# High and low parts of a row in one 512-column product: every other up chunk of a second feed-forward

## Chip, core and metric

One core of a Trainium2 chip runs the whole program. The metric is device time in microseconds of one execution, as the median of several runs. The engines that matter here are TensorE (products, with a weight load ahead of each; PE and PEld in the profile), VectorE (DVE), ScalarE (ACT) and SyncE (SP), whose queue starts the loads from memory.

## What is computed

A decoder trunk of two layers on 256 positions of width 1024, in float32. Each layer has a token mixer and a gated feed-forward, both with a normalised and modulated input and a gated residual. The feed-forward, cut to what matters:

```python
def swiglu(h, w_gate_up, w_down):           # 1024 -> 2 x 2816 -> 1024
    g, u = jnp.split(h @ w_gate_up, 2, axis=-1)
    return (jax.nn.silu(g) * u) @ w_down

h = modulate(x, norm_ffn[i], sh_f, sc_f)    # rms_norm(x) * (1 + scale) + shift
x = x + g_f[:, None, :] * swiglu(h, w_gate_up[i], w_down[i])
```

Layer 0 has an attention as its mixer, layer 1 a short gated convolution. The change is in the feed-forward of layer 1, called `f1` in the tiles' names.

## The kernel before

Everything lies with features on the 128 partitions and the 256 positions along a row (`S = 256`); the width of 1024 is 8 blocks k (`KD = 8`) of 128. To keep float32 precision on an engine format with fewer bits, each operand is split into a high part (rounded copy, ScalarE, L98 for weights) and a low part (the remainder, VectorE, L99). A product of weights and rows is then three products into one accumulator, `mm3`: high weights with high rows (L254), high weights with low rows (L255), low weights with high rows (L258). Each has its own weight load of 128x128 and moves 256 columns.

Weights come in chunks of 256 output columns. `prep` loads a chunk into one of five `wf` buffers and splits it into `wh` and `wl`, of which there are three each; `get` runs two chunks ahead of the products, so the split of a chunk waits until an older chunk's products are done. Between the weight chunks `ada_piece` computes modulation vectors on VectorE (L109). A scheduler sets the order of the instructions on each engine from the code's order and from the priorities; SyncE's queue takes the loads in the code's order.

The feed-forward, `ffn(l, norm, av, done)`, runs over 11 chunks j of 256 hidden features. For j = 0 gate and up run together from a row that isn't normalised yet (`raw_gemm`); its up accumulators are the two PSUM banks tagged "alt", its gate accumulators two of the four tagged "gemm". For j = 1 to 10, `feat_gemm` gives the gate accumulator `pg` and then the up accumulator `pu`, each 8 k x 2 halves o x 3 products, one bank of 2 x 256 columns. ScalarE takes the silu of `pg` (L456), VectorE multiplies it with `pu` (L458), and `split` stores high and low parts in `a1h` and `a1l` (L405, L406). `out_proj` then makes the down products `op_d`: 8 accumulators x 22 blocks x 3 products. Residuals and stores follow.

The rows that gate and up products read are `hs`, a pair of tiles for high and low parts with rows 1 KB apart. `new_pair("h", ...)` takes the pair anew for each of the four norms (`m0`, `f0`, `m1`, `f1`), in the same two places.

Two things stand ahead of the plain chunks of some stages: `settle` issues two tiny bfloat16 products at the end of `raw_gemm`, and the argument `cuts` of `feat_gemm` divides some low-weight products of one chunk in two.

Of the kernel before, what the change touches and what calls it, by code (L numbers as in the profile page):

```python
# [8 lines left out]
F32 = mybir.dt.float32  # L9
F32R = mybir.dt.float32r  # L10
BF16 = mybir.dt.bfloat16
AF = mybir.ActivationFunctionType
# [3 lines left out]
P = 128  # L16
S = 256
D = 1024
KD = D // P
# [14 lines left out]
def trunk_kernel(ctx: ExitStack, tc: tile.TileContext, out_in, x_t, cols_in, scale_in, shift_in, ada_in, qk_rows, kv_in,  # L34
                 o_in, in_in, gu_in, down_in, out_f):
    nc = tc.nc
# [3 lines left out]
    act = ctx.enter_context(tc.tile_pool(name="act", bufs=1))  # L40
    tmp = ctx.enter_context(tc.tile_pool(name="tmp", bufs=2))
    psum = ctx.enter_context(tc.tile_pool(name="psum", bufs=1, space=bass.MemoryType.PSUM))

    def ps_gemm(name):
        return psum.tile([P, 2, CW], F32, tag="gemm", name=name, bufs=4)
# [7 lines left out]
    def ps_alt(name):  # L53
        return psum.tile([P, 512], F32, tag="alt", name=name, bufs=2)
# [90 lines left out]
    def room(tag, n, name, dtype=F32):  # L145
        size = {"al": KF * S + 16, "ah": KF * S, "zh": KD * (S + 32), "zl": KD * (S + 2)}.get(tag, KD * S)
        return act.tile([P, size], dtype, tag=tag, name=name)[:, 16 if tag == "al" else 0:][:, :n]

    def pair_rows(flat):
        return flat.rearrange("p (k s) -> p k s", s=S)  # L150

    def new_pair(tag, name, nk):
        return tuple(pair_rows(room(tag + p, nk * S, name + p, F32R)) for p in "hl")

    room("al", 1, "first_al")
    xT = act.tile([P, KD, S], F32, name="xT")
    hs = new_pair("h", "m0", KD)
    room("ah", 1, "first_ah")
    x_tok = room("zh", 2 * D, "x_tok").rearrange("p (t d) -> p t d", d=D)
    for t in range(2):  # L160
# [76 lines left out]
    def produce(upto):  # L237
        while pos[0] < len(chunks) and pos[0] <= upto:
            ch = chunks[pos[0]]
            if ch[0] == "a":  # L240
                ada_piece(*ch[1:])
            else:
                ready[ch[1]] = prep(ch[2], ch[3], "_".join(map(str, ch[1])), ch[1] in first_two)
            pos[0] += 1

    def get(key):
        n = place[key]
        produce(order[min(n + AHEAD, len(order) - 1)])
        return ready.pop(key)


    def mm3(ps, lhs, rhs, first, last, cut=0):
        (ah, al), (bh, bl) = lhs, rhs
        nc.tensor.matmul(ps, ah, bh, start=first, stop=False, skip_group_check=True)  # L254
        nc.tensor.matmul(ps, ah, bl, start=False, stop=False, skip_group_check=True)  # L255

        for a, b in ((0, cut), (cut, S)) if cut else ((0, None),):
            nc.tensor.matmul(ps[:, a:b], al, bh[:, a:b], start=False, stop=last, skip_group_check=True)  # L258

    def feat_gemm(parts, xs, nk, cuts=()):  # L260

        cuts = list(cuts)
        xh, xl = xs
        for k in range(nk):
            for ps, (wh, wl) in parts:
                for o in range(2):
                    cs = slice(o * P, (o + 1) * P)
                    mm3(ps[:, o], (wh[:, k, cs], wl[:, k, cs]), (xh[:, k], xl[:, k]),
                        k == 0 and o == 0, k == nk - 1, cuts.pop(0) if o and k % 2 and cuts else 0)

    def tok_gemm(parts, xs, nk, between={}):
        xh, xl = xs
        for k in range(nk):
            for fn, *args in between.get(k, ()):
                fn(*args)
            for ps, (wh, wl) in parts:
                for t in range(2):
                    ts = slice(t * P, (t + 1) * P)
                    mm3(ps[:, t], (xh[:, k, ts], xl[:, k, ts]), (wh[:, k], wl[:, k]),
                        k == 0 and t == 0, k == nk - 1)  # L280
# [6 lines left out]
    def wide_pair(name):  # L287
        flat = [room("z" + p, RAW, name + p, F32R) for p in "hl"]
        return (tuple(f[:, :KD * S].rearrange("p (k s) -> p k s", s=S) for f in flat),
                tuple(f.rearrange("p (k s) -> p k s", s=S + 2) for f in flat))  # L290
# [12 lines left out]
    def modulated_tile(hs, l, sh, scl, rows, k, name):  # L303
        t = tmp.tile([P, S], F32, tag="t", name="t_" + name, bufs=3)
        nc.vector.scalar_tensor_tensor(t, xT[:, k], mcol(l, scl, k), rows, op0=ALU.mult, op1=ALU.mult)
        nc.scalar.activation(hs[0][:, k], t, AF.Identity, bias=mcol(l, sh, k))
        nc.vector.scalar_tensor_tensor(hs[1][:, k], t, mcol(l, sh, k), hs[0][:, k].bitcast(F32),
                                       op0=ALU.add, op1=ALU.subtract)

    def modulated(l, sh, scl, rows, name):  # L310
        hs = new_pair("h", name, KD)
        for k in range(KD):
            modulated_tile(hs, l, sh, scl, rows, k, f"{name}_{k}")
        return hs
# [89 lines left out]
    def split(dst, k, src, name, psum_src=False):  # L404
        nc.scalar.activation(dst[0][:, k], src, AF.Copy)  # L405
        nc.vector.tensor_sub(dst[1][:, k], src, dst[0][:, k].bitcast(F32))  # L406
# [7 lines left out]
    def raw_gemm(keys, norm, name):  # L414


        raw = norm.raw
        pss = [[psum.tile([P, S + 2], F32, tag=tag, name=f"raw_{name}_{i}{o}", bufs=n) for o in range(2)]
               for i, (tag, n) in enumerate((("gemm", 4), ("alt", 2)))]
        ws = [get(k) for k in keys]  # L420
        for k in range(KD):
            if k == 3:
                norm.rstd()
            if k == 4:
                rows = norm.rows()
                with tc.high_priority(400):
                    hs = modulated(norm.l, norm.sh, norm.scl, rows, name)
            for ps, (wh, wl) in zip(pss, ws):
                for o in range(2):
                    cs = slice(o * P, (o + 1) * P)  # L430
                    mm3(ps[o], (wh[:, k, cs], wl[:, k, cs]), (raw[0][:, k], raw[1][:, k]), k == 0, k == KD - 1)
        settle(name)
        res = []
        for i, tag in enumerate("sa"):
            y = tmp.tile([P, 2, S], F32, tag=tag, name=f"rawy_{name}_{i}")
            b = tmp.tile([P, 2], F32, tag="rawb", name=f"rawb_{name}_{i}")
            for o in range(2):
                nc.vector.tensor_copy(b[:, o:o + 1], pss[i][o][:, S:S + 1])
                nc.vector.tensor_mul(y[:, o], pss[i][o][:, :S], rows)
            res.append((y, b))  # L440
        return res[0], res[1], hs

    def ffn(l, norm, av, done):
        for j in range(KF // 2):
            if j == 0:
                (s, bs), (a, ba), hs = raw_gemm([("g", l, j), ("u", l, j)], norm, f"f{l}")
                for o in range(2):
                    nc.scalar.activation(s[:, o], s[:, o], AF.Silu, bias=bs[:, o:o + 1])
                    nc.vector.scalar_tensor_tensor(a[:, o], a[:, o], ba[:, o:o + 1], s[:, o], op0=ALU.add,
                                                   op1=ALU.mult)  # L450
            else:
                pg, pu = ps_gemm(f"pg_{l}_{j}"), ps_gemm(f"pu_{l}_{j}")
                feat_gemm([(pg, get(("g", l, j)))], hs, KD, (128, 64, 192, 96) if (l, j) == (0, 1) else ())
                feat_gemm([(pu, get(("u", l, j)))], hs, KD)
                s = tmp.tile([P, 2, S], F32, tag="s", name=f"s_{l}_{j}")
                nc.scalar.activation(s, pg, AF.Silu)  # L456
                a = tmp.tile([P, 2, S], F32, tag="a", name=f"a_{l}_{j}")
                nc.vector.tensor_mul(a, s, pu)  # L458
            split(av, slice(2 * j, 2 * j + 2), a, f"{l}_{j}")
        out_proj([[(("d", l, j, i), n) for i, n in enumerate((8, 8, 6))] for j in range(4)], av, l, G_F, done)  # L460

# [14 lines left out]
    def mod_columns(y, name):  # L476

        ps = ps_misc(f"mod_c_{name}")
        n = y.shape[1] // P
        for i in range(n):  # L480
            nc.tensor.matmul(ps[:, i:i + 1], y[:, i * P:(i + 1) * P], firsts, start=True, stop=True)
        return ps[:, :n]
# [16 lines left out]
    def normed(k):  # L499
        t = tmp.tile([P, S], F32, tag="t", name=f"t_m0_{k}", bufs=3)  # L500
        nc.vector.scalar_tensor_tensor(t, xT[:, k], mcol(0, SC_M, k), rows0, op0=ALU.mult, op1=ALU.mult)
        return t
# [51 lines left out]
    with tc.manual_schedule(engines={mybir.EngineType.PE, mybir.EngineType.DVE, mybir.EngineType.Activation}):  # L554
# [13 lines left out]
        for k in range(KD):  # L568
            nc.tensor.matmul(c_ps[k // 4][:, k % 4 * P:][:, :P], sc[:, k:k + 1].to_broadcast([P, P]), ident, start=True,
                             stop=True)  # L570
# [17 lines left out]
        ps = mod_columns(y, "sc0")  # L588
# [3 lines left out]
        t = normed(0)  # L592
# [7 lines left out]
        for k in range(KD):  # L600
# [18 lines left out]
            if n < KD:  # L619
# [3 lines left out]
                t = normed(n)  # L623
# [100 lines left out]
    ov, _ = wide_pair("ov")  # L724
# [50 lines left out]
    for j in range(4):  # L775
# [7 lines left out]
        else:  # L783
            pc, pu = ps_gemm(f"pc_{j}"), ps_gemm(f"pu_{j}")
# [9 lines left out]
        with tc.high_priority(400):  # L794
            for o in range(2):
                k = 2 * j + o
# [82 lines left out]
```

## Time and profile before

| | |
|---|---|
| time, median of 3 runs | 586.41 us (585.92 to 586.62) |
| span of the profiled execution | 584.2 us |
| its own time beside the span | not listed by the profile; the median lies 2.2 us above the span |
| TensorE, products | 577.0 us busy, 99% of the span, 5026 products |
| VectorE | 454.8 us, 78% |
| ScalarE | 315.7 us, 54% |
| loads and stores | 156.04 MB, mean 267 GB/s |
| granted TensorE clock, mean | 0.999 |

Busy time of products overlaps from one to the next, so a busy TensorE isn't yet one at its best; the distance from start to start says more. In the rows, `pu<-f1h,wh_u` reads: accumulator `pu`, from the rows `f1h` and the weights `wh_u`. A row of the timeline gives start, duration, engine, line, instruction, tiles and shapes. In the table of stretches the columns are the stretch, then busy microseconds and the number of instructions of PE, PEld, DVE, ACT and POOL, the granted clock, the share of the DMA engines and GB/s.

### The profile page before, as it was taken

Reading aid. Unit: us, or ns where it says so; the run is one execution under the profiler, and the core shown is the slowest. Engines: PE = TensorE matmul, PEld = TensorE weight load, DVE = VectorE, ACT = ScalarE, POOL = GpSimd, SP = SyncE. Lnnn points to the kernel's source line nnn. Section 1 sums busy time; section 2 is a strip of 40 time slices with the busy share of each in tenths; the row PEclk is TensorE's granted clock in tenths of the full one; section 3 lists DMA queues with packets and bytes.
Section 4 is the critical chain, followed back from the end, with each engine's and each line's share of the span. In section 5 each row is a group of like instructions: output and inputs, shape, how many; then the busy total and the mean of one; then the engine's idle time right before and its main releaser. Section 6 shows DMA issues by size and latency. Waiting matters only on the chain.

```text
span 584.2 us, 12010 instructions
## 1 busy us (share of the span) xinstructions
PE 577.0 (99%) x5026; PEld 569.4 (97%) x5026; DVE 454.8 (78%) x722; ACT 315.7 (54%) x526; POOL 1.1 (0%) x8
## 2 busy tenths in 40 slices
PE   8999999999999999999999999999999999999997
PEld 6899999999999999999999999999999999999997
DVE  5789989998999799877977999759976576555550
ACT  6457889597644454534446745546745345443330
POOL 0000000000000000000000000000000000000000
PEclk9999999999999999999999999999999999999999
DMA  8999999855898898877995379737387666655400
GB/s 321 391 380 402 347 337 350 336 194 196 308 402 334 309 378 354 286 272 273 362 344 195 119 289 367 263 118 267 142 312 256 212 254 220 237 172 203 143 20 18
DMA packets 25109, 156.04 MB, mean 267 GB/s; under 512 B 2784, under 2 KB 3168, under 8 KB 8928
## 3 DMA queue, kind: packets, MB, share of 16 engines
q1 hardware_dynamic: 25056, 155.28, 71.6%
q8 instruction: 39, 0.64, 0.4%
q14 instruction: 14, 0.11, 0.0%
HBM read 154.22 MB, written 1.05 MB: 266 GB/s over the span
## 4 chain that ended last, share of the span: by engine, by line
PE 94%; DMA 2%; DVE 2%; issue 1%; SPq 0%; ACT 0%; DVEq 0%; ACTq 0%
PE pu L255 7%; PE pu L254 7%; PE pu L258 7%; PE op_d L258 7%; PE op_d L255 7%; PE op_d L254 7%; PE pg L254 6%; PE pg L255 6%; PE pg L258 6%; PE raw_f L254 1%; PE op_o L258 1%; PE raw_f L255 1%; PE op_o L255 1%; PE raw_f L258 1%; PE pb L254 1%; PE pb L258 1%
## 5 line engine op out<-in xcount | busy, mean ns | idle before, releaser
L109 DVE SCALAR_TENSOR_TENSOR prod<-wa,c_all 128x1024 f32<-128x1024 f32 x80 | 97.8, 1222 | 12.3 <-DMA wa<-in_ada_dram 11.3
L98 ACT ACTIVATE wh_d<-wf_d 128x1024 fp32r<-128x1024 f32 (+1 forms) x48 | 45.3, 981 | 63.5 <-issue 42.4
L99 DVE TENSOR_TENSOR wl_d<-wf_d,wh_d 128x1024 fp32r<-128x1024 f32 (+1 forms) x48 | 52.9, 1133 | 24.4 <-ACT wh_d L98 24.3
L98 ACT ACTIVATE wh_g<-wf_g 128x1024 fp32r<-128x1024 f32 x44 | 45.6, 1052 | 44.4 <-issue 44.0
L98 ACT ACTIVATE wh_u<-wf_u 128x1024 fp32r<-128x1024 f32 x44 | 44.5, 1051 | 38.0 <-issue 35.9
L99 DVE TENSOR_TENSOR wl_u<-wf_u,wh_u 128x1024 fp32r<-128x1024 f32 x44 | 52.4, 1222 | 14.6 <-ACT wh_u L98 14.3
L99 DVE TENSOR_TENSOR wl_g<-wf_g,wh_g 128x1024 fp32r<-128x1024 f32 x44 | 53.5, 1222 | 2.6 <-ACT wh_g L98 2.5
L254 PE MATMUL op_d<-a0h,wh_d 128*128 128x256 f32 x176 | 48.6, 276 | 0.0
L255 PE MATMUL op_d<-a0l,wh_d 128*128 128x256 f32 x176 | 48.6, 276 | 0.0
L258 PE MATMUL op_d<-a0h,wl_d 128*128 128x256 f32 x176 | 48.6, 276 | 0.0
L254 PE MATMUL op_d<-a1h,wh_d 128*128 128x256 f32 x176 | 48.6, 276 | 0.0
L255 PE MATMUL op_d<-a1l,wh_d 128*128 128x256 f32 x176 | 48.6, 276 | 0.0
L258 PE MATMUL op_d<-a1h,wl_d 128*128 128x256 f32 x176 | 48.6, 276 | 0.0
L254 PE MATMUL pg<-f0h,wh_g 128*128 128x256 f32 x160 | 44.5, 278 | 0.0
L258 PE MATMUL pg<-f0h,wl_g 128*128 128x256 f32 (+3 forms) x164 | 44.4, 275 | 0.0
L254 PE MATMUL pg<-f1h,wh_g 128*128 128x256 f32 x160 | 44.2, 277 | 0.0
L255 PE MATMUL pg<-f0l,wh_g 128*128 128x256 f32 x160 | 44.2, 276 | 0.0
L254 PE MATMUL pu<-f0h,wh_u 128*128 128x256 f32 x160 | 44.2, 276 | 0.0
L255 PE MATMUL pu<-f0l,wh_u 128*128 128x256 f32 x160 | 44.2, 276 | 0.0
L258 PE MATMUL pu<-f0h,wl_u 128*128 128x256 f32 x160 | 44.2, 276 | 0.0
L255 PE MATMUL pg<-f1l,wh_g 128*128 128x256 f32 x160 | 44.2, 276 | 0.0
L258 PE MATMUL pg<-f1h,wl_g 128*128 128x256 f32 x160 | 44.2, 276 | 0.0
(294 smaller groups left out, 2022.4 us busy)
## 6 DMA issues: line engine op xcount, KB each, us to landing
wa<-in_ada_dram SPq DMA_DIRECT2D x40, 1024.0 KB, 5.5
wf_g<-in_gate_up_dram SPq DMA_DIRECT2D x22, 1024.0 KB, 5.0
wf_u<-in_gate_up_dram SPq DMA_DIRECT2D x22, 1024.0 KB, 4.9
wf_d<-in_down_dram SPq DMA_DIRECT2D x16, 1024.0 KB, 5.0
wf_d<-in_down_dram SPq DMA_DIRECT2D x8, 768.0 KB, 5.0
wa_sc<-in_scale_dram SPq DMA_DIRECT2D x8, 512.0 KB, 7.2
wa_sh<-in_shift_dram SPq DMA_DIRECT2D x8, 512.0 KB, 8.1
wf_qk<-in_qk_rows_dram SPq DMA_DIRECT2D x8, 512.0 KB, 6.9
```

Of the source, the lines that this page charges most:

```text
L98: nc.scalar.activation(wh[:, a:b], wf[:, a:b], AF.Copy)
L99: nc.vector.tensor_sub(wl[:, a:b], wf[:, a:b], wh[:, a:b].bitcast(F32))
L109: nc.vector.scalar_tensor_tensor(t, w, 1.0, c_all, op0=ALU.mult, op1=ALU.mult, accum_out=dst)
L254: nc.tensor.matmul(ps, ah, bh, start=first, stop=False, skip_group_check=True)
L255: nc.tensor.matmul(ps, ah, bl, start=False, stop=False, skip_group_check=True)
L258: nc.tensor.matmul(ps[:, a:b], al, bh[:, a:b], start=False, stop=last, skip_group_check=True)
```

## The change

The pair of tiles for the normed rows becomes one tile `hp` of 8 rows with 2 x 256 columns: a row's high part and, right behind it, its low part; rows are now 2 KB apart, and the tile is made once and used by all four norms. In layer 1's feed-forward, chunks j = 1, 3, 5, 7 and 9 make their up products with `feat_gemm2`: for each k and half o one product of the high weights with the 512 columns of both parts, into a whole bank, and one of the low weights with the 256 columns of the high part, into the bank's left half. In chunks 1, 5 and 9 the low weights come first, in 3 and 7 the high ones. The two halves o have a bank each, both tagged "alt". After that ScalarE copies the right half of each bank out, VectorE adds the left half, and VectorE multiplies with the silu. All other products are as before.

```diff
     xT = act.tile([P, KD, S], F32, name="xT")
-    hs = new_pair("h", "m0", KD)
+    hp = act.tile([P, KD, 2, S], F32R, name="hp")
+    hs = hp[:, :, 0], hp[:, :, 1]
...
+    def feat_gemm2(pss, w, nk, low_first):
+
+        wh, wl = w
+        for k in range(nk):
+            for o in range(2):
+                cs = slice(o * P, (o + 1) * P)
+                ps = pss[o].rearrange("p (a s) -> p a s", s=S)
+                for low in (low_first, not low_first):
+                    if low:
+                        nc.tensor.matmul(ps[:, 0], wl[:, k, cs], hp[:, k, 0], start=k == 0 and low_first,
+                                         stop=k == nk - 1 and not low_first, skip_group_check=True)
+                    else:
+                        nc.tensor.matmul(ps, wh[:, k, cs], hp[:, k], start=k == 0 and not low_first,
+                                         stop=k == nk - 1 and low_first, skip_group_check=True)
...
     def modulated(l, sh, scl, rows, name):
-        hs = new_pair("h", name, KD)
...
-                pg, pu = ps_gemm(f"pg_{l}_{j}"), ps_gemm(f"pu_{l}_{j}")
+                split_up = l == 1 and j % 2
+                pg, pu = ps_gemm(f"pg_{l}_{j}"), None if split_up else ps_gemm(f"pu_{l}_{j}")
                 feat_gemm([(pg, get(("g", l, j)))], hs, KD, (128, 64, 192, 96) if (l, j) == (0, 1) else ())
-                feat_gemm([(pu, get(("u", l, j)))], hs, KD)
+                if split_up:
+                    pus = [ps_alt(f"pu_{l}_{j}_{o}") for o in range(2)]
+                    feat_gemm2(pus, get(("u", l, j)), KD, j % 4 == 1)
+                else:
+                    feat_gemm([(pu, get(("u", l, j)))], hs, KD)
...
-                nc.vector.tensor_mul(a, s, pu)
+                if split_up:
+                    for o in range(2):
+                        b = tmp.tile([P, S], F32, tag="t", name=f"pub_{l}_{j}_{o}", bufs=3)
+                        nc.scalar.activation(b, pus[o][:, S:], AF.Copy)
+                        nc.vector.tensor_add(b, b, pus[o][:, :S])
+                        nc.vector.tensor_mul(a[:, o], s[:, o], b)
+                else:
+                    nc.vector.tensor_mul(a, s, pu)
```

On TensorE, from the last products of chunk 1's gate on, the order before is (names carry a chunk's number and a buffer's):

```order
L254 MATMUL pg_1_5303<-f1h,wh_g_1_5126 128x256
L255 MATMUL pg_1_5303<-f1l,wh_g_1_5126 128x256
L258 MATMUL pg_1_5303<-f1h,wl_g_1_5127 128x256
L254 MATMUL pu_1_5304<-f1h,wh_u_1_5134 128x256
L255 MATMUL pu_1_5304<-f1l,wh_u_1_5134 128x256
L258 MATMUL pu_1_5304<-f1h,wl_u_1_5135 128x256
```

and now, on the same engine at the same place:

```order
L255 MATMUL pg_1_5296<-hp,wh_g_1_5121 128x256
L256 MATMUL pg_1_5296<-hp,wh_g_1_5121 128x256
L259 MATMUL pg_1_5296<-hp,wl_g_1_5122 128x256
L281 MATMUL pu_1_0_5353<-hp,wl_u_1_5130 128x256
L284 MATMUL pu_1_0_5353<-hp,wh_u_1_5129 128x512
L281 MATMUL pu_1_1_5354<-hp,wl_u_1_5130 128x256
L284 MATMUL pu_1_1_5354<-hp,wh_u_1_5129 128x512
```

Three products of 256 columns became one of 256 and one of 512, here with the low weights first; TensorE's list has 80 rows fewer (4732 for 4812), and nothing else in it moved.

On VectorE, where chunk 1's up products are taken out of PSUM and the next weights are split, the order before is:

```order
L99 TENSOR_TENSOR wl_u_2_5364<-wf_u_2_5361,wh_u_2_5363 128x1024
L458 TENSOR_TENSOR a_1_5419<-s_1_5417,pu_1_5304 128x512
L99 TENSOR_TENSOR wl_g_3_5428<-wf_g_3_5425,wh_g_3_5427 128x1024
L406 TENSOR_TENSOR a1l<-a_1_5419,a1h 128x512
L99 TENSOR_TENSOR wl_g_3_5428<-wf_g_3_5425,wh_g_3_5427 128x1024
```

and now, on VectorE at the same place:

```order
L99 TENSOR_TENSOR wl_u_2_5358<-wf_u_2_5355,wh_u_2_5357 128x1024
L482 TENSOR_TENSOR pub_1_0_5398<-pub_1_0_5398,pu_1_0_5353 128x256
L482 TENSOR_TENSOR pub_1_1_5402<-pub_1_1_5402,pu_1_1_5354 128x256
L483 TENSOR_TENSOR a_1_5397<-s_1_5395,pub_1_0_5398 128x256
L483 TENSOR_TENSOR a_1_5397<-s_1_5395,pub_1_1_5402 128x256
L99 TENSOR_TENSOR wl_g_3_5413<-wf_g_3_5410,wh_g_3_5412 128x1024 x2
L421 TENSOR_TENSOR a1l<-a_1_5397,a1h 128x512
```

Four instructions stand for one, and both halves of the next low gate weights moved ahead of the split of chunk 1's result. On ScalarE two copies (`pub_1_0`, `pub_1_1`) stand after the silu of chunk 1, ahead of the next weights' high parts. SyncE's and GpSimd's lists are the same as before.

## Prediction

> **What bounds the kernel now.** I read the page first (share of the span by engine, then the chain of work that ended last), then the waits of the matmul engine, then the stretches of the second layer's feed-forward, and last single matmuls in the timeline.
>
> ```profile
> span 584.2 us, 12010 instructions
> PE 577.0 (99%) x5026; PEld 569.4 (97%) x5026; DVE 454.8 (78%) x722; ACT 315.7 (54%) x526; POOL 1.1 (0%) x8
> ...
> PE 94%; DMA 2%; DVE 2%; issue 1%; SPq 0%; ACT 0%; DVEq 0%; ACTq 0%
> ```
>
> TensorE is busy for 99% of the span and holds 94% of the chain. Its busy rows overlap (a product is shown as some 276 ns, far longer than the step to the next), so what counts is the step from start to start. Next, who keeps it waiting, and the stretches of the second feed-forward (gate and up products, down products, what follows the last product):
>
> ```profile
> PE warm L543 <- DVE ident_r L555: 1.8, 1, 1.8
> PE mod_ps_sh L469 <- DMA wa_sh<-in_shift_dram: 0.9, 1, 0.9
> PE mod_ps_sh L469 <- DVE mod L492: 0.3, 1, 0.3
> PE pq L255 <- DVE m0l L506: 0.2, 1, 0.2
> PE mod_ps_sc L469 <- DMA wa_sc<-in_scale_dram: 0.2, 1, 0.2
> ...
> 412.00:521.00 109.00, 109.00 (x965) 109.00 (x963) 74.74 (x92) 54.42 (x68) 0.00 (x0) 1.00 0.64 229
> 521.00:580.80 59.80, 59.80 (x528) 59.60 (x526) 25.89 (x29) 18.85 (x21) 0.00 (x0) 1.00 0.31 109
> 580.80:584.20 3.40, 0.00 (x0) 0.00 (x0) 0.48 (x1) 0.00 (x0) 0.00 (x0) 0.90 0.11 39
> ```
>
> None of the five waits is for a tile of a feed-forward (warm, the mod tiles and pq belong to the start of the kernel). From 412 to 580.8 us it never pauses, at full granted clock (the 1.00), while VectorE works 74.74 of 109 us and ScalarE 54.42. So this stage lasts as long as its products take, and the change has to be priced in steps of TensorE. The step comes from starts a known number of products apart:
>
> ```profile
> 504.48 0.28 PE L254 MATMUL pu<-f1h,wh_u 128*128 128x256 f32 x1
> ...
> 509.92 0.28 PE L254 MATMUL pg<-f1h,wh_g 128*128 128x256 f32 x1
> ...
> 113.00 0.28 PE L255 MATMUL op_o<-ovl,wh_o 128*128 128x256 f32 x1
> ...
> 124.78 0.28 PE L254 MATMUL op_o<-ovh,wh_o 128*128 128x256 f32 x1
> ...
> 144.10 0.28 PE L255 MATMUL pg<-f0l,wh_g 128*128 128x256 f32 x1
> ...
> 145.16 0.28 PE L255 MATMUL pg<-f0l,wh_g 128*128 128x256 f32 x1
> ```
>
> The first two rows bound one chunk of up products of the second layer: 48 products (8 k, 2 halves, 3 each) in 5.44 us, 113.3 ns each. In the attention's output projection 100 products take 11.78 us, 117.8 ns each, and in the first gate chunk of the first layer 9 take 1.06 us, again 117.8. So a 256-column product has two cadences, both held over long rows without a wait. The second layer's feed-forward is in the fast one from its first gate chunk to its end. I call them fast (113.3) and slow (117.8).
>
> **The change, part by part.** Five chunks (j = 1, 3, 5, 7, 9) are touched, each with 8 k and 2 halves: 80 groups. A group was three products of 256 columns with three weight loads: 3 x 113.3 = 340 ns. It becomes one of 256 (low weights) and one of 512 columns (high weights) with two loads. The columns streamed stay 768.
>
> *The 512-column product.* No product of this kind is in the trace. Nearest are the float32 products of attention, where 256 columns take a double pass:
>
> ```profile
> 82.75 0.43 PE po L729 x2
> ...
> 69.80 0.60 PE L696 MATMUL s<-qkT 128*128 128x256 f32 x2
> 70.04 0.47 PE L697 MATMUL s<-mask_r,ident_r 128*128 128x256 f32 x1
> 70.35 0.28 PE L254 MATMUL pv<-wh_v,m0h 128*128 128x256 f32 x1
> ```
>
> The first row is from the chain: two such products hold it for 0.43 us, 215 ns each, their weight loads wholly inside. I take 215 for 512 columns. Its lower bound is that row too; its upper bound is two fast products, 226.6 ns, if the step went by columns alone.
>
> *The 256-column product beside it.* The last three rows show a 256-column product (L697) after such a pair: from the pair's start to the product after L697 is 0.55 us; less 0.43 for the pair, 0.12 us are left for L697. That is the slow cadence or a little under. The lower bound is what weight loads alone allow, seen where a product is cut in two and the loads can't hide:
>
> ```profile
> 143.76 0.36 PE L258 MATMUL pg<-f0h,wl_g 128*128 128x64 f32 x2
> ...
> 143.87 0.19 PEld L254 LDWEIGHTS pg<-f0h,wh_g 128*128 128x128 f32 x1
> 143.98 0.19 PEld L255 LDWEIGHTS pg<-f0l,wh_g 128*128 128x128 f32 x1
> ```
>
> Two loads follow each other in 0.11 us, 110 ns. So this product takes 110 to 117.8 ns. I take 115, between the fast cadence of its own stage and the 0.12 of the row that has a long product ahead of it.
>
> Sum of a group: 215 + 115 = 330 ns against 340, 10 ns less; over 80 groups 0.8 us less. Ends: 215 + 110 = 325 gives 1.2 us less; 226.6 + 117.8 = 344.4 gives 0.35 us more.
>
> By the Trainium skill (page "TensorE: Matmul & The Clock Gate", section "Back-to-back issue gap") a warm product steps by its columns at 2.4 GHz plus about 2.5 ns, which is 109.2 ns for 256 columns and 215.8 for 512; dropping a product would then be worth 2.5 ns, 0.2 us in all, an estimate from that page. The 113.3 ns here is 4 ns over its figure for 256 columns, so the trace doesn't bear that rule out for paired loads and products.
>
> *The evacuation.* One VectorE product of 128x512 (0.69 us) becomes two additions and two products of 128x256, and ScalarE gets two copies out of PSUM. Rows for these and for the deadline behind them, at the end of chunk 1:
>
> ```profile
> 406.45 0.38 ACT L363 ACTIVATE rrow_n<-rr_n 128x256 f32<-128x256 f32 x1 [1.61 <-PE rr_n L300]
> ...
> 416.73 0.42 DVE L439 TENSOR_TENSOR rawy_f<-raw_f,rrow_n 128x256 f32<-128x256 f32 x1
> ...
> 423.14 0.69 DVE L458 TENSOR_TENSOR a<-s,pu 128x512 f32<-128x512 f32 x1
> 425.85 1.22 DVE L99 TENSOR_TENSOR wl_g<-wf_g,wh_g 128x1024 fp32r<-128x1024 f32 x1
> 429.55 2.36 DVE L99 TENSOR_TENSOR wl_u<-wf_u,wh_u 128x1024 fp32r<-128x1024 f32 x2
> ...
> 433.75 0.28 PE L254 MATMUL pg<-f1h,wh_g 128*128 128x256 f32 x1
> 439.19 0.28 PE L254 MATMUL pu<-f1h,wh_u 128*128 128x256 f32 x1
> ```
>
> VectorE gets 4 x 0.42 - 0.69 = 1.0 us more per changed chunk, ScalarE 2 x 0.38 = 0.8. Queued behind them are the next weights' splits: the low gate weights of chunk 3 end at 427.07 and are needed at 433.75 (6.7 us to spare), the low up weights end at 431.91 and are needed at 439.19 (7.3 us). The additions wait for ScalarE's copies, which adds under 1 us once. So I cost this at nothing; without that cover it would be 5 x 1.0 us. SyncE's and GpSimd's rows don't change.
>
> *The accumulators.* Up products of changed chunks go to the two "alt" banks. Chunk 0 uses these just before: their last reader is the 416.73 row, free at 417.15.
>
> ```profile
> 417.44 0.28 PE L254 MATMUL pu<-f1h,wh_u 128*128 128x256 f32 x1
> ```
>
> TensorE reaches chunk 1's up products at 417.44, 0.29 us later, and the second bank one group later, 0.6 us after it is free. Hidden; if VectorE were late by more, TensorE would stand for the difference once. Later changed chunks come 21.8 us after the last use.
>
> *The shared tile.* High and low rows now lie 2 KB apart in one tile that all four norms reuse, where two tiles were taken anew each time. The readers of one stage end before the next writes, so no new wait; a row's 256 columns stay contiguous. No row shows a pitch other than 1 KB. I take nothing, with the difference of the cadences (4.5 ns) per product that reads it as the bound either way.
>
> The sum: span 584.2 - 0.8 = 583.4 us. The span stands 2.2 us under the median of 586.41, which holds the work around it; so 586.41 - 0.8 = **585.6 us**. A measurement of this kernel tells about 0.2% (1.17 us) from no change, so the forecast is "no change that can be told".
>
> **The rivals.**
> 1. *The cadence slips.* The broken rhythm leaves the plain products behind a changed chunk in the slow cadence. For it: the rows at 144.10 and 113.00 lie behind short or long products, and slow. Against it: chunk 1 of this stage became fast behind short products, and holds. Price: from chunk 9 to the end there are 96 gate and up and 528 down products, 624 x 4.5 ns = 2.8 us; between changed chunks 4 x 144 products, 2.6 us. With the 0.8 gained, the last stretch alone gives 588.4, all of them 591.0. It turns the sign once over 180 products are slow, and measurably from some 440.
> 2. *A clean 512 stream.* The 256-column product after it steps at the loads' 110 ns: 1.2 us less, 585.2. For it: nothing but the loads is left to wait for; against it: no 256-column row steps below 113.
> 3. *The change doesn't do what it says.* The step goes by columns: 226.6 + 113.3 = 340, and the time stays at 586.4 (586.8 with the slow cadence). Against it: the 215 ns row.
> 4. *A late evacuation or bank* makes TensorE wait at chunk 1, or starves a weight split: some tenths at the bank, up to 5 us without cover. Against it: the 6.7 us above.
>
> **How the numbers follow.** Forecast (fast cadence kept, group 327 to 334 ns): 0.52. Rival 2: 0.15. Rival 1: 0.22, most of it beyond the bound. Rival 3: 0.08. Rival 4 and the pitch: 0.03. Rival 2 lies at the bound, and the forecast's lower end near it, so faster gets 0.22; slower has rivals 1 and 4 less the small slips, 0.23; the rest, 0.55, is no change. The range takes the spread of the three runs below 585.2 and reaches to one slip of the last stretch: 584.9 to 588.4. The forecast's own range is 585.1 to 586.1.
>
> **What would show it.** Right: the changed chunk of up products takes 16 x 330 = 5.28 us instead of 5.44, the plain chunks after it keep 5.44, the weight splits still end microseconds ahead, and no wait of TensorE appears at 417 us. Wrong: 5.65 us per plain chunk after a changed one (rival 1), a changed chunk of 5.2 (rival 2) or 5.44 us (rival 3), or idle time of TensorE at its first up product (rival 4).

## The result, and the profile after

The changed kernel takes 592.24 us (median of four runs, 591.06 to 592.32), the kernel before 586.16 us (four runs, 585.0 to 586.62): a ratio of 1.0099 with a 95% interval of 1.0077 to 1.012. It is slower by 6.1 us, where 585.6 us had been forecast and 588.4 us was the top of the range.

The first view is the head of the page, and below it the two stretches of the second feed-forward (gate and up products, then down products; the columns are those of the view before):

```profile
span 590.4 us, 11876 instructions
PE 584.0 (99%) x4946; PEld 572.7 (97%) x4946; DVE 457.5 (77%) x737; ACT 318.8 (54%) x536; POOL 1.1 (0%) x8
```

```profile
412.00:524.70 112.70, 112.70 (x883) 109.18 (x883) 78.16 (x107) 57.48 (x77) 0.00 (x0) 1.00 0.61 221
524.70:590.40 65.70, 62.35 (x530) 62.14 (x528) 26.37 (x30) 18.92 (x21) 0.00 (x0) 1.00 0.30 102
```

There are 80 products fewer, and TensorE is busy 7 us longer, at a full granted clock. The span grew by 6.2 us (590.4 against 584.2). TensorE has five waits, all at the start of the kernel and none for a tile of the feed-forward; this is the longest, and the other four are 0.2 or 0.3 us each:

```profile
PE warm L570 <- DVE ident_r L582: 1.8, 1, 1.8
```

So the time is in the steps of the products themselves. The timeline of TensorE shows the moment at which it changes, the start of chunk 1's up products, and then the starts of the chunks that follow (the first column is the start):

```profile
417.51 0.28 PE L281 MATMUL pu<-hp,wl_u 128*128 128x256 f32 x1
417.62 0.39 PE L284 MATMUL pu<-hp,wh_u 128*128 128x512 f32 x1
417.85 0.28 PE L281 MATMUL pu<-hp,wl_u 128*128 128x256 f32 x1
417.97 0.40 PE L284 MATMUL pu<-hp,wh_u 128*128 128x512 f32 x1
...
423.15 0.28 PE L255 MATMUL pg<-hp,wh_g 128*128 128x256 f32 x1
...
428.80 0.28 PE L255 MATMUL pu<-hp,wh_u 128*128 128x256 f32 x1
...
434.46 0.28 PE L255 MATMUL pg<-hp,wh_g 128*128 128x256 f32 x1
...
440.11 0.39 PE L284 MATMUL pu<-hp,wh_u 128*128 128x512 f32 x1
...
445.69 0.28 PE L255 MATMUL pg<-hp,wh_g 128*128 128x256 f32 x1
```

Up to 417.62 a product follows in 0.11 us. The first 512-column product takes 0.23 us to the next start (417.62 to 417.85), which is two fast steps and no gain. From there on the 256-column products beside it take 0.12 and the 512-column products 0.23 to 0.24. Chunk 1's up products last 5.64 us (417.51 to 423.15) instead of 5.44, those of chunk 3 5.58 (440.11 to 445.69); of the other three, chunks 5 and 9 take 5.58 and chunk 7 takes 5.66. The order of the weights doesn't explain this: it is low first in 1, 5 and 9, high first in 3 and 7. And each plain chunk in between takes 5.65 us (423.15 to 428.80, 428.80 to 434.46), 48 products of 117.8 ns: the slow cadence, which the plain products keep to the end.

The sum closes. The five changed chunks take 28.04 us instead of 27.20, 0.84 more. Behind the first of them lie 1200 plain products (9 gate chunks and 5 up chunks of 48, 528 down products), at 4.5 ns each 5.4 us. Together 6.2 us, the whole difference of the spans.

What had been costed at nothing does lie beside other work. These are VectorE's weight splits behind the additions and products of chunk 1:

```profile
424.83 2.35 DVE L99 TENSOR_TENSOR wl_g<-wf_g,wh_g 128x1024 fp32r<-128x1024 f32 x2
...
430.12 2.36 DVE L99 TENSOR_TENSOR wl_u<-wf_u,wh_u 128x1024 fp32r<-128x1024 f32 x2
```

The low gate weights of chunk 3 are ready at 427.18 and used at 434.46, the low up weights at 432.48 and 440.11: more than 7 us to spare in both.

### The profile page after: what moved, and what is told of

Same layout as the page of the kernel before. It is cut to its first block, busy times and chain, and to the rows that moved or that the text cites. A ratio compares the mean times of both kernels' runs of the same rounds, so it can differ in the third digit from the quotient of the medians.

```text
span 590.4 us, 11876 instructions
## 1 busy us (share of the span) xinstructions
PE 584.0 (99%) x4946; PEld 572.7 (97%) x4946; DVE 457.5 (77%) x737; ACT 318.8 (54%) x536; POOL 1.1 (0%) x8
## 4 chain that ended last, share of the span: by engine, by line
PE 67%; DVE 16%; DMA 13%; issue 4%; ACT 1%; SPq 0%; DVEq 0%; ACTq 0%
DMA wa<-in_ada_dram 11%; DVE prod L109 4%; PE op_d L256 4%; PE op_d L255 4%; PE op_d L259 3%; PE pg L255 3%; PE pg L256 3%; PE pg L259 3%; PE pu L284 3%; DVE wl_u L99 3%; PE pu L259 3%; PE pu L255 3%; PE pu L256 3%; DVE wl_g L99 2%; DVE wl_d L99 2%
## 5 line engine op out<-in xcount | busy, mean ns | idle before, releaser
L255 PE MATMUL pg<-hp,wh_g 128*128 128x256 f32 x320 | 89.2, 279 | 0.0
L259 PE MATMUL pg<-hp,wl_g 128*128 128x256 f32 (+1 forms) x324 | 89.1, 277 | 0.0
L256 PE MATMUL pg<-hp,wh_g 128*128 128x256 f32 x320 | 88.9, 278 | 0.0
L255 PE MATMUL pu<-hp,wh_u 128*128 128x256 f32 x240 | 66.6, 277 | 0.0
L256 PE MATMUL pu<-hp,wh_u 128*128 128x256 f32 x240 | 66.5, 277 | 0.0
L259 PE MATMUL pu<-hp,wl_u 128*128 128x256 f32 x240 | 66.5, 277 | 0.0
L259 PEld LDWEIGHTS pg<-hp,wl_g 128*128 128x128 f32 x324 | 60.5, 188 | 0.0
L256 PEld LDWEIGHTS pg<-hp,wh_g 128*128 128x128 f32 x320 | 60.1, 188 | 0.1
L255 PEld LDWEIGHTS pg<-hp,wh_g 128*128 128x128 f32 x320 | 60.1, 188 | 0.1
```

## The experiments

The theory after the result: a product of another length than 256 columns ends TensorE's fast cadence, and nothing restores it. The rivals: the alternating banks and the order of halves do it, or the 2 KB pitch, or the evacuation; or each product behind a changed chunk is slowed for a reason of its own. Runs told as single have one profiled execution and no interval. Unless said otherwise an edit is made to the changed kernel.

**The 512-column product as two of 256** (`e1_narrow`). Banks, order, halves, tile and evacuation stay.

```diff
-                        nc.tensor.matmul(ps, wh[:, k, cs], hp[:, k], start=k == 0 and not low_first,
-                                         stop=k == nk - 1 and low_first, skip_group_check=True)
+                        for a in range(2):
+                            nc.tensor.matmul(ps[:, a], wh[:, k, cs], hp[:, k, a],
+                                             start=k == 0 and not low_first and a == 0,
+                                             stop=k == nk - 1 and low_first, skip_group_check=True)
```

> As the changed kernel in banks, order and evacuation, but each 512-column product is made as two of 256 columns (high rows into the left half, low rows into the right half of the bank). Theory W (a 512-column product itself breaks the fast cadence of 113.3 ns): no slip, all chunks of the second feed-forward at 5.44 us, 586.2 to 586.6 us. Theory O (the order of high and low, the two banks in turn or the halves break it): slow cadence of 117.8 ns from chunk 1 on, 591 to 592 us.

Measured: 585.72 us against 585.8, a ratio of 1.0003 (0.9984 to 1.0021). The timeline at chunk 1:

```profile
417.20 0.28 PE L281 MATMUL pu<-hp,wl_u 128*128 128x256 f32 x1
417.31 0.39 PE L285 MATMUL pu<-hp,wh_u 128*128 128x256 f32 x2
...
422.64 0.28 PE L255 MATMUL pg<-hp,wh_g 128*128 128x256 f32 x1
```

The chunk takes 5.44 us and so do all that follow. The pitch, the shared tile, the second pair of banks, the order of the weights and the longer evacuation together cost nothing that can be measured. What is left as the cause of the loss is the length of the product.

**Only chunk 9 changed** (`e2_only_chunk9`).

```diff
-                split_up = l == 1 and j % 2
+                split_up = l == 1 and j == 9
```

> Only chunk 9 has the wide products. Theory W: chunks 1 to 8 keep 5.44 us, chunk 9 takes 5.6, and the 624 products after it run at 117.8 ns: 624 x 4.5 = 2.8 us and 0.15 in the chunk, 589.1 us. If the slip needs chunk 1's place (the low weights first after the first gate chunk, banks just freed): no slip, 586.3 us.

Measured: 589.96 us, ratio 1.0065 (1.0048 to 1.0082). The starts of chunk 9's up products, chunk 10's gate products and its up products:

```profile
505.36 0.28 PE L281 MATMUL pu<-hp,wl_u 128*128 128x256 f32 x1
...
511.00 0.28 PE L255 MATMUL pg<-hp,wh_g 128*128 128x256 f32 x1
...
516.65 0.28 PE L255 MATMUL pu<-hp,wh_u 128*128 128x256 f32 x1
```

All plain chunks up to 505.36 run at 113.3 ns. Then 5.64 us for the changed chunk, 5.65 for the plain one, and 117.8 ns to the end. One changed chunk near the end thus loses the 2.8 us that rival 1 gave its last stretch, and 0.2 us in itself. Together that is 3.0 us of the 3.8 by which the span (588.0) is above the kernel before's; the rest was there when the chunk began (505.36 against 504.48), in stages that the edit doesn't touch.

**Ways back to the fast cadence** (`e3_resets`, a single run). Tiny products behind four changed chunks, and four cut products (as the kernel has them in the first layer) in gate chunk 8. The tiny products go into a bank that nothing reads.

```diff
+                    if j in (1, 3, 5, 9):
+                        tiny({1: 1, 3: 2, 5: 3, 9: 4}[j], f"{j}")
...
-(128, 64, 192, 96) if (l, j) == (0, 1) else ()
+(128, 64, 192, 96) if (l, j) in ((0, 1), (1, 8)) else ()
```

> The changed kernel with a different break after each changed chunk: one tiny bfloat16 product after chunk 1, two after 3, three after 5, gate products of chunk 8 cut in two at four places after chunk 7, four tiny ones after chunk 9. Theory W with a cadence that is a state set anew at every break: some of the five stretches go back to 113.3 ns, others stay at 117.8; each stretch won saves 0.65 us, the last one 2.8 us, so 587 to 592 us. If the slow cadence came from what the chunks leave behind on other engines (weights, banks): all stretches stay at 117.8, 592 us.

Measured: 592.7 us. One to four tiny products change nothing: the products after them step at 117.8 ns. The cuts do. The last of them and the first product after it:

```profile
496.96 0.35 PE L259 MATMUL pg<-hp,wl_g 128*128 128x96 f32 x2
497.14 0.32 PE L255 MATMUL pu<-hp,wh_u 128*128 128x256 f32 x1
...
502.62 0.28 PE L255 MATMUL pg<-hp,wh_g 128*128 128x256 f32 x1
```

The last cut, into 96 and 160 columns, ends the slow stretch, where behind each of the three cuts ahead of it the products had settled at 117 to 120 ns again (up chunk 8 takes 5.48 us, its first step of 0.15 included), and the 512-column products of chunk 9 start it again (down products at 117.8 ns). So it is a condition that lasts, not a price that each product pays.

**What a product costs by itself** (`e4_probe`, a single run). No up product is changed; behind the up products of chunks 2, 4, 6 and 8 stand 32 extra products of one kind each, into a bank that nothing reads: added work, nothing left out.

```diff
-                split_up = l == 1 and j % 2
+                split_up = False
...
+            if j == 2:
+                nc.tensor.matmul(ps, ident_r, hp[:, i % KD], start=True, stop=True, skip_group_check=True)
+            elif j == 6:
+                nc.tensor.matmul(ps[:, 0], ws[0], ws[1][:, 0], start=True, stop=True, skip_group_check=True)
+            elif j == 8:
+                nc.tensor.matmul(ps, ws[0], ws[1], start=True, stop=True, skip_group_check=True)
...
```

> The shared tile stays, no chunk has wide up products; 32 products extra after the up products of chunks 2, 4, 6 and 8, each into a scratch bank with its own weight load: float32r of 512 columns, float32r of 384, bfloat16 of 256, bfloat16 of 512. If a float32r product steps by columns (113.3 / 256 = 0.443 ns each): 227 and 170 ns; if it steps by columns at full speed plus a part per weight load: 220 and 167. Bfloat16: 109 and 216 ns if the rest over full speed is the float32r rows' own, 113 and 220 if it is the weight load's. Time up by 32 x (227 + 170 + 113 + 220) = 23 us, more if the stretches after turn slow. The chunks before the first probe at 5.44 us if the shared tile and its pitch cost nothing.

Measured: 616.37 us. The first row of the two float32r groups, each with the gate product behind it:

```profile
434.90 1.56 PE L441 MATMUL probe<-hp,ident_r 128*128 128x512 f32 x6
...
442.35 0.28 PE L255 MATMUL pg<-hp,wh_g 128*128 128x256 f32 x1
464.97 5.76 PE L448 MATMUL probe<-hp,ident_r 128*128 128x384 f32 x32
470.56 0.28 PE L255 MATMUL pg<-hp,wh_g 128*128 128x256 f32 x1
```

and of the two bf16 groups the rows that give the first and the last start:

```profile
L443 PE MATMUL probe<-x_b,w_b x32: 272/273/283, 493.2 to 496.6; 128*128 128x256 bf16 x32
L445 PE MATMUL probe<-x_b,w_b x32: 379/379/390, 519.3 to 526.0; 128*128 128x512 bf16 x32
```

In float32r, 32 products of 512 columns take 7.45 us, 233 ns each (the first 226, the others 230 to 236), and of 384 columns 5.59 us, 175 each. In bf16, 31 steps of 256 columns take 3.4 us, the first 120 ns and the others 108 to 110, and 31 of 512 columns 6.7 us, the first 226 and the others 215 to 216. The 215 that the prediction took for 512 columns does exist, in another type. The Trainium skill (page "TensorE: Matmul & The Clock Gate", section "Back-to-back issue gap") has 109.2 and 215.8 ns by the formula that it gives for a product by itself: that agrees with the bf16 steps here, and not with the float32r steps of 113.3 or 117.8 and of 226 to 236. Up to 434.90 the chunks run at 113.3, from there to the end at 117.8; 32 bf16 products in a row don't restore the cadence either.

**Which lengths break it** (`e6_widths`, then `e8_widths_clean`, single runs). One extra float32r product behind the up products of a chunk, again into a bank that nothing reads; no up product is changed. In the first run one cut stands in each gate chunk that follows, in the second four.

```diff
-                split_up = l == 1 and j % 2
+                split_up = False
...
+                if l == 1 and j in widths:
+                    one_product(widths[j], f"{j}")
...
+    widths = {1: 512, 2: 384, 3: 320, 4: 272, 5: 258, 6: 240, 7: 192, 8: 128, 9: 64}     (first run)
+    widths = {1: 258, 2: 320, 3: 240, 4: 192, 5: 64, 6: 272, 7: 0, 8: 256}               (second run)
```

> No wide up products; one extra float32r product into a scratch bank after the up products of chunks 1 to 9, of 512, 384, 320, 272, 258, 240, 192, 128 and 64 columns, and a cut of 96 and 160 columns late in each gate chunk from 2 on, to go back to the fast cadence. Theory W (only a longer product breaks it): slow from the extra product to the cut for 512 to 258 columns, no change for 240 to 64. Theory N (any product of another length than 256 breaks it): slow after all nine. Both need the cut to reset: then up chunks 2 to 10 run at 113.3 ns. Time: 9 x 0.1 for cuts, 1.1 for products, some 33 slow products per break, 588 to 590 us.

> No wide up products; extra products after the up products of chunks 1 to 8: one of float32r with 258, 320, 240, 192, 64 and 272 columns, two tiny bfloat16 ones, and, as a control, one of float32r with 256 columns; after chunk 9 none. All gate chunks from 2 on have the four cuts (128, 64, 192, 96), so that each extra product meets the fast cadence. Theory N (any product of another length than 256 breaks it): the 11 products after each extra one are slow, but for the 256 control. Theory W (only longer ones do): fast after 240, 192, 64 and the tiny ones. If the cuts lead into the fast cadence from a slow one alone, the up chunks of 9 and 10 are slow. Time: 0.5 us per cut chunk, 590 to 591 us.

Measured: 593.7 and 599.16 us. In the first run the cut often failed, so that several lengths came upon a cadence that was slow already and tell nothing. The two kinds of rows, a length that breaks it (first run) and the control of 256 columns (second run):

```profile
422.77 0.39 PE L433 MATMUL one<-hp,ident_r 128*128 128x512 f32 x1
423.00 0.28 PE L255 MATMUL pg<-hp,wh_g 128*128 128x256 f32 x1
423.12 0.28 PE L256 MATMUL pg<-hp,wh_g 128*128 128x256 f32 x1
```

```profile
510.79 0.28 PE L436 MATMUL one<-hp,ident_r 128*128 128x256 f32 x1
510.90 0.28 PE L255 MATMUL pg<-hp,wh_g 128*128 128x256 f32 x1
511.01 0.28 PE L256 MATMUL pg<-hp,wh_g 128*128 128x256 f32 x1
```

One single 512-column product is enough: the next steps are 0.12. Of the lengths that came upon the fast cadence, 512, 384, 320, 272, 258, 240, 128 and 64 all ended it, and 256 did not. Two columns more or sixteen fewer do as much as 256 more. The length of 192 and the two tiny products came upon a slow cadence and stay untested.

The second run shows also that a cut can work either way. The four cuts of the first layer's gate chunk 1, which no edit touches, are into 128 and 128, 64 and 192, 192 and 64, and 96 and 160 columns. They began there in the fast cadence, where in the kernel before they begin in the slow one, and left it slow. Below are the first and the last of ten plain products between the second cut and the third, the same between the third and the fourth, and the ends of that feed-forward:

```profile
143.80 0.28 PE L256 MATMUL pg<-hp,wh_g 128*128 128x256 f32 x1
...
144.82 0.28 PE L256 MATMUL pg<-hp,wh_g 128*128 128x256 f32 x1
...
145.28 0.28 PE L256 MATMUL pg<-hp,wh_g 128*128 128x256 f32 x1
...
146.34 0.28 PE L256 MATMUL pg<-hp,wh_g 128*128 128x256 f32 x1
...
146.64 0.32 PE L255 MATMUL pu<-hp,wh_u 128*128 128x256 f32 x1
...
316.28 0.28 PE L255 MATMUL raw_m<-zvh,wh_cg 128*128 128x258 f32 x1
```

Nine steps take 1.02 us behind the first two cuts (113.3 ns) and 1.06 us behind the third (117.8): cuts into 128 and 128 and into 64 and 192 kept the fast cadence, 192 and 64 ended it, and 96 and 160 did not bring it back. In the second layer the control of 256 columns was followed by the same. Of the eight other gate chunks with four cuts, all of which began slow, six left it fast; the two behind 240 and 272 columns were fast after their first cut and slow again from the third. So the finding on lengths holds for single products: two halves that make up 256 columns can leave the fast cadence as it is.

From 146.64 to 316.28 the first feed-forward takes 169.6 us; in the kernel before it is 163.2 (146.98 to 310.22). Of this run's 13 us above the kernel before, 6.4 come from a cadence that its own edit did not set.

**One cut behind each changed chunk** (`e5_cut_after`), in the gate chunk that follows; and the same with the low weights first in all changed chunks (`e10_low_first_cut`).

```diff
+    def split_next(l, j):
+        return l == 1 and j % 2 == 0
...
-(128, 64, 192, 96) if (l, j) == (0, 1) else ()
+(128, 64, 192, 96) if (l, j) == (0, 1) else (96,) if split_next(l, j) else ()
...
-                    feat_gemm2(pus, get(("u", l, j)), KD, j % 4 == 1)
+                    feat_gemm2(pus, get(("u", l, j)), KD, True)     (second kernel alone)
```

> The changed kernel, and in the gate chunk after each changed chunk one low product is cut into 96 and 160 columns (in the first layer and in the resets run the fast cadence began right after such a cut). Theory W (the 0.17 us per changed chunk and the slow stretches after it are the whole loss): all plain chunks and the down products back at 5.44 us per 48 products, changed chunks still 5.6; per changed chunk 0.17, 12 slow products 0.05 and the cut some 0.1 us, so 5 x 0.32 = 1.6 us over before, 587.4 us. If the cut alone doesn't reset: 592.5 us.

> The changed kernel with the low weights first in all five changed chunks and one cut of 96 columns in each gate chunk after them (that cut worked after chunks with low weights first, and failed after chunks 3 and 7 with high weights first). If the order ahead of it decides: all plain stretches at 113.3 ns; changed chunks 5.64, gate chunks with a cut 5.60, so 5 x (0.20 + 0.16) = 1.8 us over before, 587.8 us. This is then the change without its slow stretches, and shows what the wide products alone are worth. If not: between 588 and 592 us.

Measured for the first: 588.92 us, ratio 1.0047 (1.0029 to 1.0065). The cut restored the fast cadence behind chunks 1, 5 and 9 (low weights first) and failed behind 3 and 7 (high weights first). Its profiled execution, at 590.5 us the longest of its four, holds a wait in the first feed-forward:

```profile
301.73 0.38 PE L259 MATMUL op_d<-a0h,wl_d 128*128 128x256 f32 x1 [0.97 <-DVE wl_d L99]
301.95 0.28 PE L255 MATMUL op_d<-a0h,wh_d 128*128 128x256 f32 x1
...
302.54 0.28 PE L259 MATMUL op_d<-a0h,wl_d 128*128 128x256 f32 x1
```

From 301.95 to 302.54 five products take 0.59 us, 118 ns each, and so it goes on to the end of that feed-forward; ahead of the wait they step at 113.3: behind this one pause the cadence was slow as well.

Measured for the second: 587.62 us, ratio 1.0027 (1.0017 to 1.0036). Its starts of chunk 1's up products, of gate chunk 2 with the cut, and of the two chunks behind:

```profile
417.17 0.28 PE L281 MATMUL pu<-hp,wl_u 128*128 128x256 f32 x1
...
422.81 0.28 PE L255 MATMUL pg<-hp,wh_g 128*128 128x256 f32 x1
...
428.41 0.28 PE L255 MATMUL pu<-hp,wh_u 128*128 128x256 f32 x1
...
433.85 0.28 PE L255 MATMUL pg<-hp,wh_g 128*128 128x256 f32 x1
```

All plain chunks and the down products are fast again. What is left is 0.20 us for each changed chunk (5.64) and 0.16 for each cut chunk (5.60): 5 x 0.36 = 1.8 us. The span is 1.5 us above the kernel before's (585.7 against 584.2), and the stage began 0.3 us earlier (417.17 against 417.44). Of these 1.8 us, 1.0 are the changed chunks and 0.8 the cuts that restore the cadence. This is the best form of the change that was run, and it still loses: with the plain chunks back in the fast cadence, the 512-column product itself is no gain.

**Four cuts in gate chunk 10** (`e9_rescue_last`), so that the down products come back to the fast cadence.

```diff
-(128, 64, 192, 96) if (l, j) == (0, 1) else ()
+(128, 64, 192, 96) if (l, j) in ((0, 1), (1, 10)) else ()
```

> The changed kernel with the four cuts (128, 64, 192, 96) in the gate chunk of chunk 10, after the last changed chunk. If the slow stretches are the loss: the up chunk of 10 and the 528 down products return to 113.3 ns, 576 x 4.5 = 2.6 us less than the changed kernel, the cut chunk 0.4 us more than a slow one, so 590.0 us. If the fast cadence isn't entered there: 592.6 us.

Measured: 589.59 us, ratio 1.0058 (1.0043 to 1.0073). The gate chunk with the cuts takes 6.05 us (513.04 to 519.09); chunk 10's up products and all down products are at 113.3 ns again. By these steps it gives back 576 products x 4.5 ns = 2.6 us, less 0.4 for the cuts (6.05 against 5.65); the span is 2.5 us under the changed kernel's.

**The cadence without the change** (`e7_cuts_moved`, a single run, on the kernel before). The four cuts of the first feed-forward and of the convolution stage are replaced by one each, and one stands in the attention's output projection.

```diff
-(128, 64, 192, 96) if (l, j) == (0, 1) else ()
+(96,) if (l, j) == (0, 1) else ()
...
-() if j else (128, 64, 192, 96))
+() if j else (96,))
...
-                        base + k == 0, base + k == total - 1)
+                        base + k == 0, base + k == total - 1,
+                        96 if keys[j][i][0] == ("o", 2) and (o, k) == (0, 3) else 0)
```

> The kernel before, without wide products, but with its slow stretches shortened: the four cuts in the first plain chunk of the first feed-forward and of the convolution become the one of 96 columns, earlier, and the third output chunk of attention gets one such cut. If a cut of 96 columns enters the fast cadence from any slow stretch: 36 products less at 4.5 ns and three cuts less (some 0.1 us each) at two places, 130 products faster in the output projection: 0.9 + 0.5, so 584.6 to 585 us. If it depends on what ran before: some of these stretches stay slow, and the long first feed-forward at 117.8 ns would cost 6.5 us, 592 us.

Measured: 594.04 us, span 592.2. None of the three single cuts led into the fast cadence. Two starts in the first feed-forward, 48 up products apart:

```profile
146.62 0.28 PE L254 MATMUL pu<-f0h,wh_u 128*128 128x256 f32 x1
...
152.28 0.28 PE L254 MATMUL pg<-f0h,wh_g 128*128 128x256 f32 x1
```

That is 5.66 us. With the first feed-forward and the convolution stage slow and the second feed-forward fast, the kernel before is 8 us longer, ten times the 0.8 us that the change had been forecast to save.

## Why the prediction was wrong

*The step that failed is the condition "fast cadence kept".* On it the sum put nothing for the plain products behind a changed chunk; 5.4 of the 6.2 us were lost there, at 117.8 ns each instead of 113.3. The bound (a stage that lasts as long as its steps of TensorE), the two cadences, and the price of the rival were read rightly: 2.6 us between the changed chunks and 2.8 behind the last is the measured 5.4. But the rival got 0.22, and the range ended at the slip of the last stretch alone, 588.4. The argument against it was "chunk 1 of this stage became fast behind short products, and holds". That showed how the cadence can begin; it "holds" there over products of 256 columns alone. The trace before had rows for both sides. Against the two slow rows that the prediction named stands this one in the k projection, behind three products of 128 columns:

```profile
63.12 0.49 PE L689 MATMUL pt<-ident,tk 128*128 128x128 f32 x3
...
63.69 0.28 PE L254 MATMUL pk<-wh_k,m0h 128*128 128x256 f32 x1
...
67.77 0.28 PE L254 MATMUL pv<-wh_v,m0h 128*128 128x256 f32 x1
```

From 63.69 to 67.77 36 products take 4.08 us, 113.3 ns each. So the rows didn't decide the rival, and a range that follows from them would have held it whole: with "all of them" it would have reached 591.0 us, still 1.2 short, because of the next step.

*The 512-column product, 215 ns.* The row it came from was one of the two that a float32 product of 256 columns makes: L729 stands once for each of 8 heads and left 16 such rows. So it was no price for 512 columns. In float32r the product of 512 columns is 226 at its first step and 229 to 237 after that: above even the upper bound of 226.6, since that bound had been made from the fast cadence. *The 256-column product beside it, 115 ns,* is 113 at its first step and 117 to 124 after that. A group takes 349 to 354 ns instead of 330, and the term "0.8 us less" became 0.84 more. Rival 3, the step by columns, had the kind right (its chance was 0.08), and `e10_low_first_cut` shows the sign: without the slip behind it a changed chunk costs 0.20 us and saves nothing.

*The evacuation, the accumulators and the shared tile,* costed at nothing, cost nothing: `e1_narrow` has all three and stands at 1.0003, and the weight splits end 7 us ahead. No wait appeared at 417 us. Rival 4 is out, and rival 2 with it, since no 256-column product of a changed chunk stepped below 113.

*What stays open.* Why a length other than 256 starts the slow cadence, and what decides whether a cut ends it. In `e5_cut_after` the order ahead of the cut went with the outcome in five of five cases, and in `e10_low_first_cut` low weights first worked five times of five; that is a correlation, not a cause. Nor is another length the only thing that changes the cadence. In the q and k projections of the kernel before, in a row of nothing but 256-column products and without a wait, it turns from fast to slow:

```profile
34.25 0.28 PE L258 MATMUL pk<-wh_qk,m0l 128*128 128x256 f32 x1
...
37.88 0.28 PE L255 MATMUL pq<-m0l,wh_qk 128*128 128x256 f32 x1
...
38.11 0.28 PE L254 MATMUL pk<-wh_qk,m0h 128*128 128x256 f32 x1
...
39.41 0.28 PE L258 MATMUL pk<-wh_qk,m0l 128*128 128x256 f32 x1
```

32 steps up to 37.88 take 3.63 us, 113.4 ns each, and 11 from 38.11 on take 1.30, 118 each; the accumulator changes between them, and no run tests whether that is the reason. The weight loads' rows start 2 to 4 ns behind their products' in both cadences, so the trace doesn't show where the 4.5 ns go. Two of ten runs of `e1_narrow` took 588.8 us and one of the kernel before beside it 589.0, without a profile; whether those 3 us are a slip of this kind isn't shown. Nor is the cause of the part of `e2_only_chunk9`'s time that lies ahead of its edit.

## What to carry to other kernels

Where a stage is a long, unbroken row of equal products, read the step from start to start over a known count, and treat it as a condition that the row keeps, not as a property of each product; an edit that puts one product of another length into the row is then priced by everything behind it, up to the next thing that changes the condition. Take a product's price from a row of its own type and length, and if there is none, let the range hold the price by columns in the slower cadence. A rival whose price is three times the expected gain belongs in the range unless a row excludes it.

## What the runs showed of the hardware

- Rows of float32r products of 256 columns, each with its own weight load, run at 113.3 or at 117.8 ns each, at a granted clock of 1.00, for hundreds of products. In the second feed-forward one product of 64, 128, 240, 258, 272, 320, 384 or 512 columns ended the fast cadence and one of 256 didn't (one trial each, 512 in several runs); a wait of 0.97 us once ended it too. In the q and k projections it also changed in a row of 256-column products alone (113.4 to 118 ns).
- A product cut into 96 and 160 columns can end the slow cadence and often didn't. Cuts into 128 and 128 and into 64 and 192 left the fast one as it was, and a cut into 192 and 64 ended it each time that it met it, all in `e8_widths_clean`.
- 512 columns of float32r in one product take 226 to 237 ns, two products of 256 columns 226.6 in the fast cadence and 235.6 in the slow one: one longer product saves an instruction and a weight load and no time against the fast cadence. In bf16 the same shape takes 215 to 216.
